# A two-layer decoder trunk: the MLP's second product by Strassen's scheme, its weight sums by adding DMAs, and the first product with the tokens in the partitions

## The chip, the cores and the metric

The kernel runs on one core of a Trainium2 chip. The metric is the device time of one execution in microseconds (us), taken as the median of several runs. TensorE (PE) multiplies, VectorE (DVE) and ScalarE (ACT) do the elementwise work, GpSimd (POOL) and SyncE (SP) mostly issue transfers. A DMA that is issued by SP is called a load here.

## The reference

256 tokens of 2048 features pass through two layers. Each layer has a mixer (gated linear attention in layer 0, windowed attention in layer 1), a cross-attention into 256 memory tokens, an output product, and an MLP; all arrays are float32. The change is in the MLP alone:

```python
def squared_relu_mlp(h, w_up, w_down):
    return jnp.square(jax.nn.relu(h @ w_up)) @ w_down
...
        x = x + squared_relu_mlp(rmsnorm(x, mlp_norm_g[i]), w_up[i], w_down[i])
```

`w_up` is 2048 x 8192 and `w_down` is 8192 x 2048, so each MLP reads 2 x 64 MB of weights.

## The kernel before, in words

Every weight is read once, in parts of 128 partitions x 1024 floats (512 KB). A part with its products is an `Item`, and the whole program is one list of items that is walked in order. In round i of the walk the load of item i + 8 is written (`load`, on SP's queue, into one of `WR` = 5 slots `wr`), then the split of item i + 3 (`split`), then the products of item i (`mm`). TensorE multiplies in a reduced form of float32, so each operand is cut into a high part and a remainder: ScalarE copies the part to `wh`, VectorE subtracts to get `wl` (four slots of each). A product of two such operands is three matmuls: high x high, high x remainder, remainder x high. As `wh` has four slots, the split of item i + 3 has to wait until TensorE is through with item i - 1.

Work that is not a product of a weight (norms, attention, transposes) sits in generators in the list `tasks`; `step_tasks` moves each of them one `yield` further in every round with products. The framework that builds the program adds all waits, and it may place an instruction on its engine elsewhere than the code has it.

The MLP of a layer runs in four quarters of 2048 hidden features. The first product has the hidden features in the partitions: `fm_halves` makes 128 of them from two items, each of 8 matmuls of 512 columns (256 tokens, high and remainder side by side) with `wh` as the weights in the array, and 8 of 256 columns with `wl`. `done` then adds the two halves (`combine`: one op of ScalarE, one of VectorE), multiplies with the norm factor, squares the positive part, and splits the result. The second product has the tokens in the partitions: `tm_halves` takes the 16 chunks of a quarter and 512 output features in 8 items of 12 matmuls each (two tiles of tokens, two chunks, three matmuls of 512 columns); at the end `add_residual` adds both banks of PSUM (the accumulators of TensorE, 8 in all: four "main", four "aux") to the residual `x`. The last 512 outputs of the last quarter are done by `last_group`, one tile of tokens after the other.

Of the kernel before, what the change touches and what calls it, by code (L numbers as in the profile page):

```python
# [28 lines left out]
# feature chunks (of 128) of the layer-0 projection, in the order of the jobs  # L29
# [20 lines left out]

class Item:
    """One load: a part of a weight with its products, or a part of an input."""

    def __init__(self, src, width, split=None, mm=None):
        self.src, self.width, self.split, self.mm = src, width, split, mm


@with_exitstack
def trunk_kernel(ctx: ExitStack, tc: tile.TileContext, a, out):
# [12 lines left out]
    # ---------------------------------------------------------------- loads  # L72
# [7 lines left out]
    gains = vec("gains", [P, 5, NK], act)     # mem, attn0, attn1, mlp0, mlp1  # L80
# [11 lines left out]
    # TensorE's clock is raised by the time the first operands are there  # L92
# [4 lines left out]
    # ------------------------------------------------------------- helpers  # L97
    def split_slot(which, name):
        return [sp.tile([P, 2 * T], F32R, tag=f"{which}{c}", name=f"{name}{c}") for c in range(NK)]

# [8 lines left out]
    class Stats:  # L109
        """1/sqrt(mean of squares + eps) of an array [token, feature]."""  # L110
# [22 lines left out]
    def spread(tok, name):  # L133
        """[token, tile] along the free axis of every partition, in PSUM."""
# [7 lines left out]
    def inv_sqrt(name, src, scale, r=None, v=None, w=None):  # L142
# [41 lines left out]
    def tm_halves(name, srcs, n, lhs, done, order=None):  # L184
        """All tokens in the partitions, n output features along the free axis."""
# [24 lines left out]
    def combine(acc, name):  # L210
        """acc's two halves added, in SBUF."""
# [6 lines left out]
    S = {}     # what later closures look up  # L218

    def put_out(c, src):  # L220
        S["os"][c] = sp.tile([P, 2 * T], F32R, tag=f"B{c}", name=f"os{c}")
# [45 lines left out]
    def x_task():  # L267
        """The residual with the tokens in the partitions."""
# [70 lines left out]
    # ---------------------------------------------------------------- layer 0  # L339
    def gla_halves():  # L340
# [29 lines left out]
        def proj_done(job, idx):  # L370
            kind, h, j = job

            def f(acc):
# [528 lines left out]
```

## Time and profile before

| what | value |
|---|---|
| time, median of 3 runs | 2143.64 us (2143.62 to 2143.68) |
| span of the profiled execution, its first to its last instruction | 2142.3 us |
| granted TensorE clock, mean over the span | 0.999 |
| read from HBM in the span | 394.52 MB |
| first product of the MLP of layer 0, first weight load into the array | 465.1 us |
| first product of layer 1's projection, first weight load into the array | 1180.8 us |

The profile describes one execution, whose own time is its span and the little before the first and after the last instruction that the profile does not show; the span is 1.3 us under the median of the runs. Busy time of TensorE counts matmuls from start to modelled end, and these overlap. The distance between the starts of equal items is therefore the better measure of what an item costs.

### The profile page before, as it was taken

The numbers are of one execution on the slowest core, as the hardware profiler recorded it, in microseconds if no ns is written. First come the engines' busy times: TensorE is split into PE (matmuls) and PEld (weight loads), VectorE is DVE, ScalarE is ACT, GpSimd is POOL, SyncE is SP. The second block draws the span as 40 slices with busy tenths as digits, with TensorE's granted clock in tenths as the row PEclk, the third lists the DMA queues.
The fourth block names the chain that finished last, engine by engine and source line by source line (L and its number), as shares of the span: only waits on it lengthen the run. The fifth ranks groups of instructions, "written<-read, shape, count | busy, mean of one in ns | idle before, by whom it ended". The sixth has DMA issues, their size and how long they took to land.

```text
span 2142.3 us, 28800 instructions
## 1 busy us (share of the span) xinstructions
PE 2129.7 (99%) x11014; PEld 1809.6 (84%) x11014; DVE 1348.5 (63%) x1971; ACT 1040.2 (49%) x1586; POOL 9.1 (0%) x26
## 2 busy tenths in 40 slices
PE   9999999999999999999999999999999999999998
PEld 9988888888888888888888887888888888888886
DVE  5655777557646656755765688567557646645673
ACT  6744666544434434434444566454444434434452
POOL 0000000000000000000000000000000000000000
PEclk9999999999999999999999999999999999999999
DMA  8855554555565555555555544555566566555572
GB/s 286 278 177 187 168 167 152 183 182 183 190 192 190 192 190 189 185 194 187 187 187 187 173 130 131 191 184 186 190 190 192 188 193 188 187 190 189 185 243 80
DMA packets 111883, 398.71 MB, mean 186 GB/s; under 512 B 12684, under 2 KB 12896, under 8 KB 111616
## 3 DMA queue, kind: packets, MB, share of 16 engines
q1 hardware_dynamic: 109872, 393.40, 56.7%
q10 hardware_dynamic: 1680, 3.38, 0.5%
q8 instruction: 86, 1.41, 0.3%
q14 instruction: 53, 0.43, 0.1%
q0 software_dynamic: 192, 0.08, 0.0%
HBM read 394.52 MB, written 2.10 MB: 185 GB/s over the span
## 4 chain that ended last, share of the span: by engine, by line
PE 99%; DMA 0%; DVE 0%; ACT 0%; SPq 0%; issue 0%; DVEq 0%
PE u_acc L175 22%; PE u_acc L176 11%; PE d_acc L203 11%; PE d_acc L202 11%; PE d_acc L201 11%; PE p_acc L175 6%; PE s_acc L175 3%; PE p_acc L176 3%; PE o_acc L201 3%; PE o_acc L202 3%; PE o_acc L203 3%; PE s_acc L176 2%; PE mk_acc L175 1%; PE v_acc L203 1%; PE v_acc L202 1%; PE v_acc L201 1%
## 5 line engine op out<-in xcount | busy, mean ns | idle before, releaser
L808 DVE TENSOR_TENSOR wl<-wr,wh 128x1024 fp32r<-128x1024 f32 (+1 forms) x734 | 890.8, 1214 | 692.9 <-ACT wh L807 691.7
L807 ACT ACTIVATE wh<-wr 128x1024 fp32r<-128x1024 f32 (+1 forms) x734 | 770.8, 1050 | 1012.6 <-issue 385.0
L175 PE MATMUL u_acc<-mx,wh 128*128 128x512 f32 x2048 | 721.0, 397 | 0.0
L176 PE MATMUL u_acc<-mx,wl 128*128 128x256 f32 x2048 | 574.8, 281 | 0.0
L175 PEld LDWEIGHTS u_acc<-mx,wh 128*128 128x128 f32 x2048 | 384.4, 188 | 92.7
L203 PE MATMUL d_acc<-wh,h 128*128 128x512 f32 x992 | 388.8, 392 | 0.0
L202 PE MATMUL d_acc<-wl,h 128*128 128x512 f32 x992 | 388.2, 391 | 0.0
L201 PE MATMUL d_acc<-wh,h 128*128 128x512 f32 x992 | 388.2, 391 | 0.0
L176 PEld LDWEIGHTS u_acc<-mx,wl 128*128 128x128 f32 x2048 | 387.1, 189 | 0.3
L202 PEld LDWEIGHTS d_acc<-wl,h 128*128 128x128 f32 x992 | 186.3, 188 | 40.8
L201 PEld LDWEIGHTS d_acc<-wh,h 128*128 128x128 f32 x992 | 186.3, 188 | 40.6
L203 PEld LDWEIGHTS d_acc<-wh,h 128*128 128x128 f32 x992 | 186.4, 188 | 40.3
L175 PE MATMUL p_acc<-ax,wh 128*128 128x512 f32 x512 | 183.8, 402 | 0.0
L176 PE MATMUL p_acc<-ax,wl 128*128 128x256 f32 x512 | 143.6, 280 | 0.0
L175 PEld LDWEIGHTS p_acc<-ax,wh 128*128 128x128 f32 x512 | 96.2, 188 | 23.7 <-ACT wh L807 1.0
L175 PE MATMUL s_acc<-ax,wh 128*128 128x512 f32 x304 | 111.3, 407 | 0.0
L201 PE MATMUL o_acc<-wh,os 128*128 128x512 f32 x256 | 100.8, 394 | 0.0
L203 PE MATMUL o_acc<-wh,os 128*128 128x512 f32 x256 | 99.6, 390 | 0.0
L202 PE MATMUL o_acc<-wl,os 128*128 128x512 f32 x256 | 99.5, 389 | 0.0
L176 PEld LDWEIGHTS p_acc<-ax,wl 128*128 128x128 f32 x512 | 96.8, 189 | 0.2
L176 PE MATMUL s_acc<-ax,wl 128*128 128x256 f32 x304 | 85.1, 280 | 0.0
L175 PEld LDWEIGHTS s_acc<-ax,wh 128*128 128x128 f32 x304 | 57.1, 188 | 15.7 <-issue 3.3
(236 smaller groups left out, 1731.8 us busy)
## 6 DMA issues: line engine op xcount, KB each, us to landing
wr<-in_w_up_dram SPq DMA_DIRECT2D x256, 512.0 KB, 4.4
wr<-in_w_down_dram SPq DMA_DIRECT2D x256, 512.0 KB, 4.4
wr<-in_w_gla_dram SPq DMA_DIRECT2D x64, 512.0 KB, 4.2
wr<-in_w_out_dram SPq DMA_DIRECT2D x64, 512.0 KB, 3.6
wr<-in_w_swa_dram SPq DMA_DIRECT2D x38, 512.0 KB, 3.7
wr<-in_w_v_dram SPq DMA_DIRECT2D x32, 388.0 KB, 4.2
wr<-in_w_mv_dram SPq DMA_DIRECT2D x16, 512.0 KB, 4.5
wr<-in_w_mk_dram SPq DMA_DIRECT2D x16, 512.0 KB, 4.3
```

The source lines that it names most:

```text
L175: pe.matmul(acc, wh[:, k * P:(k + 1) * P], rk, start=kk == 0, stop=False, skip_group_check=True)
L176: pe.matmul(acc[:, T:2 * T], wl[:, k * P:(k + 1) * P], rk[:, 0:T], start=False, stop=kk == NK - 1, skip_group_check=True)
L201: pe.matmul(acc, hi, h, start=first, stop=False)
L202: pe.matmul(acc, hi, l, start=False, stop=False)
L203: pe.matmul(acc, lo, h, start=False, stop=last)
L807: act.activation(hi[i][:, 0:w], r[:, 0:w], AF.Copy)
L808: dve.tensor_tensor(lo[i][:, 0:w], r[:, 0:w], hi[i][:, 0:w].bitcast(F32), ALU.subtract)
```

## The change

The first product now has the tokens in the partitions as well. `up(n)` makes 512 hidden features for both tiles of tokens from 8 items of 12 matmuls; ScalarE applies the norm factor and the relu (`p`). A generator, `hid_task`, then transposes the result on TensorE (8 blocks of 128 x 128 for each n, 16 n for each layer), squares it on the way out of PSUM, and, for the first seven eighths of the hidden features, makes the sums of blocks that Strassen's scheme (in Winograd's form) wants: S3, GG, S2 and S4 beside A11, A12 and A22. All seven operands of such a unit are split in one op of ScalarE and one of VectorE of 1792 elements each.

The second product runs in eighths e of 1024 hidden features (two units each). For e = 0 to 6 `down_fast(e)` makes seven products of blocks in place of eight: 7 operands x 2 units x 2 pairs of output groups are 28 items, each of 6 matmuls, where the kernel before has 16 items of 12 for the same features. Two banks per pair hold running sums for a whole layer, and after each operand one of the two banks is added to or subtracted from one block of `x` (`take`, 14 in each eighth, written two rounds with products later by `later`). The weights' sums are made in SBUF: a tile `chain` gets block B11 by a load; after its split POOL issues a DMA with `accum_op=ADD` that adds B12 to it (T1), after the next split one that adds B22 (T2), then B21 (T4). T3 is a load of B12 and an adding DMA of B22 into a slot of `wr`. Each eighth has 16 loads of 512 KB and 16 adding DMAs of 512 KB for its second product. The last eighth is done without the scheme (`down_plain`, `last_group`).

The items of the first product for the next eighth are woven into those of the second product (`woven`: 16 up items and 28 down items, the last 4 of them at the end). `WR` is 6, tiles with the tag `B` live in the pool of the phase, the pool of layer 1's mixer is opened later, and the scratch space for DMA descriptors is set to 8192. The weights are laid out anew on the host.

```diff
-WR = 5
+WR = 6
...
+A21, A11, A22, A12, S3, GG, S2, S4 = range(8)
+FAST = [(A11, "B11", 0, True, [(0, 0, 1)]),
+        (GG, "T1", 1, True, [(1, 1, -1)]),
+        (S2, "T2", 0, False, [(0, 1, -1)]),
+        (S4, "B22", 1, False, [(0, 1, -1)]),
+        (S3, "T3", 0, False, [(1, 1, -1)]),
+        (A22, "T4", 0, False, [(1, 0, 1)]),
+        (A12, "B21", 1, True, [(0, 0, 1)])]
...
         def up(n):
...
+            def part(i):
+                def mm(wh, wl):
+                    if i == 0:
+                        if n == 0:
+                            open_phase()
+                        st["acc"] = [bank("main" if n < 2 else "aux", f"u{layer}{n}_acc{t}") for t in range(2)]
+                    for t in range(2):
+                        for k in range(2):
+                            rk = S["xs"][2 * i + k]
+                            h, l = wh[:, k * 512:(k + 1) * 512], wl[:, k * 512:(k + 1) * 512]
+                            hi, lo = rk[:, t * P:(t + 1) * P], rk[:, T + t * P:T + (t + 1) * P]
+                            acc = st["acc"][t]
+                            pe.matmul(acc, hi, h, start=2 * i + k == 0, stop=False)
+                            pe.matmul(acc, hi, l, start=False, stop=False)
+                            pe.matmul(acc, lo, h, start=False, stop=2 * i + k == NK - 1)
+                    if i == 7:
+                        p = S["phase"].pool.tile([P, 2, 512], F32, tag="relu", name=f"p{layer}{n}", bufs=2)
+                        for t in range(2):
+                            act.activation(p[:, t, :], st["acc"][t], AF.Relu, scale=S["st"].tok[:, t:t + 1])
+                        making[n] = hid_task(n, p)
+                        tasks.append(making[n])
+                return Item(a["w_up"][layer, n, i], 1024, mm=mm)
...
+        def hid_task(n, p):
+            pool = S["phase"].pool
+            yield
+            yield
+            q = pool.tile([P, 8, T], F32, tag="sq", name=f"q{layer}{n}", bufs=1)
+            for o in (0, 2):
+                b = bank("aux", f"h{layer}{n}{o}")
+                for j in range(2):
+                    t, half = {A21: (1, 0), A11: (0, 0), A22: (1, 1), A12: (0, 1)}[o + j]
+                    for c in range(2):
+                        col = (2 * half + c) * P
+                        pe.transpose(b[:, j * T + c * P:j * T + (c + 1) * P], p[:, t, col:col + P], ident)
+                act.activation(q[:, o:o + 2, :].rearrange("p o c -> p (o c)"), b, AF.Square)
+            yield
+            yield
+            u = pool.tile([P, 7, 512], F32R, tag="hid", name=f"hid{layer}{n}", bufs=3)
+            if n // 2 < 7:
+                dve.tensor_tensor(q[:, S3:GG + 1, :], q[:, A11:A22 + 1, :], q[:, A21:A21 + 1, :].to_broadcast([P, 2, T]),
+                                  ALU.subtract)
+                dve.scalar_tensor_tensor(q[:, S2, :], q[:, GG, :], -1.0, q[:, A11, :], ALU.mult, ALU.subtract)
+                dve.scalar_tensor_tensor(q[:, S4, :], q[:, S2, :], -1.0, q[:, A12, :], ALU.mult, ALU.subtract)
+                first, ops = 1, 7
+            else:
+                first, ops = 0, 4
+            act.activation(u[:, 0:ops, 0:T], q[:, first:first + ops, :], AF.Copy)
+            dve.tensor_tensor(u[:, 0:ops, T:2 * T], q[:, first:first + ops, :], u[:, 0:ops, 0:T].bitcast(F32),
+                              ALU.subtract)
+            unit[n] = u
+            del making[n]
...
+            def item(idx, u, pair):
+                o, name, which, first, uses = FAST[idx]
+                def mm(wh, wl):
+                    if u == 0 and pair not in sums:
+                        sums[pair] = {}
+                    if u == 0 and which not in sums[pair]:
+                        sums[pair][which] = bank("main", f"d{layer}{e}{pair}{which}")
+                    acc = sums[pair][which]
+                    products(acc, 2 * e + u, o, wh, wl, first and u == 0, u == 1)
+                    if u == 1:
+                        def take():
+                            for t, col, sign in uses:
+                                dst = x[t][2 * pair + col]
+                                if sign > 0:
+                                    dve.tensor_tensor(dst, acc, dst, ALU.add)
+                                else:
+                                    dve.tensor_tensor(dst, dst, acc, ALU.subtract)
+                        later.append([1, take])
...
+                def plus(other):
+                    def f():
+                        pool_e.dma_start(held[pair, u], block(pair, u, other), accum_op=ALU.add)
+                    return f
+                if name == "B11":
+                    it = Item(block(pair, u, "B11"), 1024, mm=mm, held=new_tile, then=plus("B12"))
+                    it.tile = held_tile
+                    return it
+                if name == "T1":
+                    return Item(None, 1024, mm=mm, held=held_tile, then=plus("B22"))
+                if name == "T2":
+                    return Item(None, 1024, mm=mm, held=held_tile, then=plus("B21"))
+                if name == "T4":
+                    return Item(None, 1024, mm=mm, held=held_tile)
+                if name == "T3":
+                    return Item(block(pair, u, "B12"), 1024, mm=mm, plus=block(pair, u, "B22"))
+                return Item(block(pair, u, name), 1024, mm=mm)
+            return [item(idx, u, pair) for idx in range(7) for u in range(2) for pair in range(2)]
...
+        def woven(us, ds, tail):
+            hs, m = [], len(ds) - tail
+            for i, u in enumerate(us):
+                hs.append(u)
+                hs += ds[m * i // len(us):m * (i + 1) // len(us)]
+            return hs + ds[m:]
+        first, second = up(0), up(1)
+        hs = first[0:6] + second[0:6] + first[6:] + second[6:]
+        for e in range(7):
+            hs += woven(up(2 * e + 2) + up(2 * e + 3), down_fast(e), 4)
+        for g in range(4):
+            if (layer, g) == (1, 3):
+                last_group(hs, len(hs) - 8)
             else:
+                hs += down_plain(g)
...
         raw[i] = wp.tile([P, 1024], F32, tag="wr", name="wr", bufs=WR)
         nc.sync.dma_start(raw[i][:, 0:h.width], h.src)
+        if h.plus is not None:
+            pool_e.dma_start(raw[i], h.plus, accum_op=ALU.add)
...
+        if h.then:
+            h.then()
```

More of the change, by code (lines that the diff above doesn't have):

```diff
@@ L98, in split_slot @@
     def split_slot(which, name):
-        return [sp.tile([P, 2 * T], F32R, tag=f"{which}{c}", name=f"{name}{c}") for c in range(NK)]
+        pool = sp if which == "A" else S["phase"].pool
+        return [pool.tile([P, 2 * T], F32R, tag=f"{which}{c}", name=f"{name}{c}") for c in range(NK)]
     def split_scaled(dst, src, g):
@@ L693, in down, with open_phase @@
-        def down(q, g):
-            def done(accs):
-                add_residual(g, accs)
-                if q == 3:
-                    finish(g)
-            return tm_halves(f"d{layer}{q}{g}", [a["w_down"][layer, q, g, i] for i in range(8)], 512,
-                             lambda: [hid[16 * q + k] for k in range(16)], done)
+        unit = {}
+        making = {}
+        wd = a["w_down"]
+        def open_phase():
+            S["phase"].close()
+            S["phase"] = Phase(f"mlp{layer}")
+            S["st"].finish()
+            if layer == 1:
+                S["gfin"] = S["phase"].pool.tile([P, D], F32, name="gfin")
+                act.dma_start(S["gfin"], a["g_fin"])
@@ new lines, in up @@
+        def up(n):
+            st = {}
+            def part(i):
[20 more added lines that the diff above has]
+                return Item(a["w_up"][layer, n, i], 1024, mm=mm)
+            return [part(i) for i in range(8)]
@@ new lines, in operand, with products @@
+        def operand(n, o, c):
+            if n in making:
+                for _ in making[n]:
+                    pass
+            if n // 2 < 7:
+                o -= 1
+            u = unit[n]
+            return u[:, o, c * P:(c + 1) * P], u[:, o, T + c * P:T + (c + 1) * P]
+        def products(acc, n, o, wh, wl, first, last):
+            for c in range(2):
+                hi, lo = operand(n, o, c)
+                h, l = wh[:, c * 512:(c + 1) * 512], wl[:, c * 512:(c + 1) * 512]
+                pe.matmul(acc, hi, h, start=first and c == 0, stop=False, skip_group_check=True)
+                pe.matmul(acc, hi, l, start=False, stop=False, skip_group_check=True)
+                pe.matmul(acc, lo, h, start=False, stop=last and c == 1, skip_group_check=True)
@@ L745, in products @@
                 return Item(None, 0, mm=mm)
-            for i in range(8):
+            for i in range(4):
                 hs.insert(at + 3 * i, fetch(i))
-            hs += [products(t, i) for t in range(2) for i in range(8)]
+            hs += [part(t, i) for t in range(2) for i in range(4)]
         def final(t):
```

132 lines of the change are left out of this document (72 added, 60 removed).

## The prediction

> **What bounds the kernel now.** I read the page first: busy times, the slices, the chain that ended last.
>
> ```profile
> span 2142.3 us, 28800 instructions
> PE 2129.7 (99%) x11014; PEld 1809.6 (84%) x11014; DVE 1348.5 (63%) x1971; ACT 1040.2 (49%) x1586; POOL 9.1 (0%) x26
> ...
> PE 99%; DMA 0%; DVE 0%; ACT 0%; SPq 0%; issue 0%; DVEq 0%
> PE u_acc L175 22%; PE u_acc L176 11%; PE d_acc L203 11%; PE d_acc L202 11%; PE d_acc L201 11%; PE p_acc L175 6%; PE s_acc L175 3%; PE p_acc L176 3%; PE o_acc L201 3%; PE o_acc L202 3%; PE o_acc L203 3%; PE s_acc L176 2%; PE mk_acc L175 1%; PE v_acc L203 1%; PE v_acc L202 1%; PE v_acc L201 1%
> ```
>
> The chain is TensorE nearly throughout, and two thirds of it are the MLP's two products (u_acc and d_acc). Next come the waits, of ScalarE, TensorE and SP.
>
> ```profile
> ACT wh L807 <- PE d_acc L203: 351.9, 214, 1.7
> PE v_acc L201 <- ACT wh L807: 2.4, 2, 1.4
> SPq L795 <- DVE wl L808: 932.7, 400, 4.7
> ```
>
> The splits wait for TensorE to free a slot, the loads wait for the splits, and TensorE waits 2.4 us in all. So a shorter TensorE program shortens the kernel, until one of the others no longer keeps up. Last, the price of an item. ScalarE's split starts once for each item, as TensorE releases it, so the distance of these rows of the timeline (start, duration) is TensorE's time for one item.
>
> ```profile
> 545.92 1.06 ACT L807 ACTIVATE wh<-wr 128x1024 fp32r<-128x1024 f32 x1 [1.46 <-issue]
> 557.23 1.06 ACT L807 ACTIVATE wh<-wr 128x1024 fp32r<-128x1024 f32 x1 [1.46 <-issue]
> ...
> 562.85 1.06 ACT L807 ACTIVATE wh<-wr 128x1024 fp32r<-128x1024 f32 x1 [1.38 <-issue]
> 568.34 1.06 ACT L807 ACTIVATE wh<-wr 128x1024 fp32r<-128x1024 f32 x1 [1.69 <-PE d_acc L203]
> ```
>
> The first two rows lie four items of the first product apart (11.31 us): 2.827 us for each. The last two lie two items of the second product apart: 2.745 us for 12 matmuls of 512 columns, 0.229 us each. Durations of single matmuls (0.39) overlap and aren't used.
>
> **TensorE's work.** The first product has 256 items in both layers (16 n, 8 parts, 2 layers), as many as before. They go from 2.827 to 2.745: -21.1 us. The second had 256 items of 2.745, or 702.7 us. It now has 14 eighths x 28 items of 6 matmuls (1.372 each) and 32 whole items: 538.0 + 87.8 = 625.8, so -76.9 us. New are 256 transposes of 128 x 128. The chain of the layer before has the same operation, eight at a time:
>
> ```profile
> 400.23 0.87 PE mx0t L656 x8
> ```
>
> 32 groups of eight at 0.87 are +27.8 us. Together -70.2 us. One woven eighth costs TensorE 16 x 2.745 + 28 x 1.372 + 2 x 0.87 = 84.1 us; the same work costs 16 x 2.827 + 16 x 2.745 = 89.2 now. **So 5.1 us is what an eighth may lose before the change is lost**, and there are 14 of them.
>
> **VectorE and ScalarE.** Rows of the groups by line (busy us, mean ns), the last with a PSUM source and a factor per row, as the new relu has:
>
> ```profile
> L808 DVE TENSOR_TENSOR wl<-wr,wh 128x1024 fp32r<-128x1024 f32 (+1 forms) x734 | 890.8, 1214 | 692.9 <-ACT wh L807 691.7
> L807 ACT ACTIVATE wh<-wr 128x1024 fp32r<-128x1024 f32 (+1 forms) x734 | 770.8, 1050 | 1012.6 <-issue 385.0 <-PE d_acc L203 351.9 <-PE o_acc L203 81.1
> L687 DVE SCALAR_TENSOR_TENSOR u_t<-u_t 128x256 f32<-128x256 f32 x128 | 54.4, 425 | 4.4
> L642 DVE TENSOR_TENSOR x<-d_acc,x 128x512 f32<-128x512 f32 x62 | 39.8, 683 | 8.0 <-PE d_acc L203 8.0
> L727 ACT ACTIVATE fh<-wr 128x512 fp32r<-128x512 f32 x16 | 9.3, 623 | 10.8 <-DMA wr<-in_w_down_dram 10.8
> L331 ACT ACTIVATE xpt<-xt 128x512 f32<-128x512 f32 x8 | 4.7, 593 | 0.0
> L291 ACT ACTIVATE mv<-mv_acc,mem_r 128x512 f32<-128x512 f32 x4 | 2.8, 688 | 1.6 <-PE mv_acc L203 1.6
> ```
>
> The sums of a unit cost VectorE one op of 512 elements and two of 256: 0.68 + 2 x 0.42 = 1.5 us. Its ops of 1792 elements aren't in the trace. Carried on in a straight line from 512 and 1024 elements they are 2.0 us on VectorE and 1.7 on ScalarE. An eighth costs VectorE 44 splits (53.4), 14 takes (9.6) and two units (7.1): 70.1 of 84.1 us, 83%. ScalarE has 44 splits (46.2) and two units with two relus, two squares and a copy each (8.5): 65%. Neither becomes the bound by its sum. But the split of an item can start only when the item four ahead is done, and takes 1.05 + 1.21 = 2.3 us. Three small items in a row leave it 4.1 us, so 1.9 in reserve; with one item of the first product among them it is 5.5 and 3.2. What goes over the reserve, TensorE waits. Three places do:
>
> The **start of each layer** has no earlier units. Unit 0 is wanted one item of the first product after its transposes, and takes 1.2 (squares) + 1.5 + 1.7 + 2.0 = 6.4 us: 3.7 late. Unit 1 has 4.1 us of cover, and is 2.3 late. For two layers +12 us; the bounds are 0 (other products are placed ahead of it) and 21 (each chain stands behind another split).
>
> The **last unit of an eighth** is made among small items. Its subtraction and a take are 2.7 us that the next split can stand behind, 0.8 over the reserve. The unit in the middle is covered by the 3.2.
>
> The **sums T3 and T4** use the same bank one after the other, and one T4 item has only one small item behind the T3 item whose take must read the bank first. If that take stands behind a split, it ends 2.3 + 0.7 us after a start for which 1.4 us are there: 1.6 late. If it stands ahead, nothing.
>
> I take 0.8 and half of 1.6 for an eighth, and as the bound below nothing. The half rests on a row:
>
> ```profile
> 557.23 1.06 ACT L807 ACTIVATE wh<-wr 128x1024 fp32r<-128x1024 f32 x1 [1.46 <-issue]
> 558.19 0.36 ACT L213 ACTIVATE u_u<-u_acc 128x256 f32<-128x256 f32 x1
> ```
>
> Here a split of the next round stands ahead of an op that the code writes first, so ops go by when their operands are there, not by the written order alone. That is 1.6 x 14 = +22 us.
>
> **DMA.** Rows by stretch of time, the share of the 16 engines and GB/s last, and the rows of issues (KB each, us to landing):
>
> ```profile
> 10.00:30.00 20.00, 20.00 (x115) 20.00 (x114) 13.71 (x22) 14.98 (x28) 0.00 (x0) 1.00 0.99 365
> 558.00:645.00 87.00, 87.00 (x381) 71.38 (x380) 44.55 (x43) 33.72 (x34) 0.00 (x0) 1.00 0.61 192
> ...
> wr<-in_w_down_dram SPq DMA_DIRECT2D x256, 512.0 KB, 4.4
> wg<-in_wg_dram POOLq DMA_DIRECT2D x4, 17.0 KB, 4.8
> ```
>
> At a share of 0.99 loads run at 365 GB/s; the MLP now takes 192. An eighth will have 32 loads (16.8 MB) and 16 adding DMAs (8.4 MB). No adding DMA is in the trace. Its lower bound is a load of the same size (factor 1): 46 + 23 = 69 us at 365 GB/s, hidden under 84.1. The upper is twice that, since it must read its destination too: 46 + 46 = 92 us, which is no longer hidden. I take 1.5 (80.5 us, nearly full): the second read is of SBUF and not of HBM, from which the 365 come. The cover ends at a factor of 1.66.
>
> A sum must also land in time. Between one split of a `chain` tile and its next lie four small and at least two other items, 11.0 us, less 2.3 for the split itself, plus 1.9 of reserve: 10.6. From the 17 KB row, 4.8 us, and 512 KB at half of 365 GB/s beside the loads, 2.9 at factor 1 and 5.7 at 2, come 7.7 to 10.5. So I cost it at nothing, and know the cover is thin: if landing takes 2 us more than the upper value, two hand-overs in each eighth lose about 4 us, 56 in all.
>
> **Other queues.** POOL has 9.1 us of work in the whole span, and an issue there is short:
>
> ```profile
> L436 POOL DMA_DIRECT2D wg<-in_wg_dram x4 | 2.1, 514 | 203.2 <-PE pre L439 203.2
> ```
>
> At half a microsecond each, the 16 of an eighth are 8 us of its 84, and hide. SP's queue has the same 512 loads for the MLP; those of a `chain` tile wait for the split of the last sum, which is long done by then. The six slots in place of five lengthen what loads can run ahead.
>
> **Sum.** 2142.3 - 70.2 + 12 + 22 = 2106.1 for the span, and with the 1.3 us by which the median lies above it, 2107.
>
> **The rivals.** *The adding DMAs become the bound* (slower). At factor 2 an eighth lasts 92 us in place of 84.1, and its small stalls vanish in that: 14 x 7.9 = 111, so 2143.6 - 70.2 + 12 + 111 = 2196. It decides from 1.66 on; 1.88 is the point of no change. For it: 0.61 of the engines' time is already taken at 192 GB/s, and 200 of plain loads with 100 of adding ones come on top of each other. Against it: 0.99 at 365 shows that the share in the MLP has waiting in it. The Trainium skill, "Collectives: The Full Stack", section "The bandwidth ceiling: the fold count and why AG ≠ RS ≠ AR", speaks for this rival: a DMA that reduces emits two read descriptors for each chunk on one ring, so it runs at half the rate of a copy, though the addition itself is free. By that rule the factor is 2 and the time 2196; no run here shows it yet.
>
> *The written order holds after all* (slower). Then a unit's copy stands on ScalarE ahead of the next split, which waits 1.5 + 1.7 us for it and 2.0 on VectorE: 5.2 against a reserve of 1.9 at the end and 3.2 in the middle of an eighth, so 3.3 + 2.0, with 1.6 for the bank 6.9. 14 x 6.9 = 97, with 21 at the starts 2191. The row of 558.19 speaks against it.
>
> *Only the landing is late*: 2107 + 56 = 2163, slower. For it, the thin cover; against it, that the 17 KB alone need 0.05 us at 365 GB/s, so the 4.8 are fixed time, part of which the bigger transfer overlaps.
>
> *Nothing is late at all*: 2143.6 - 70.2 = 2073. For it, 2.4 us of waiting in all of TensorE's rows now; against it, VectorE at 83% where it has 63 now.
>
> **How the numbers follow.** Forecast with the stall-free case 0.56 (its own range 2073 to 2135), the adding DMAs 0.27, the written order 0.08, late landing 0.09. The range 2073 to 2205 takes in all of them; outside stay adding DMAs beyond a factor of 2 (at 3 an eighth takes 115 us, and the kernel over 2500) and a gain beyond TensorE's sum. A measurement of this kernel tells 0.2% from no change, about 4.3 us, so faster is below 2139.3 and slower above 2147.9. Of the forecast 0.54 lies below; of the DMA case 0.02 lies below and 0.03 near no change, where the factor falls between 1.66 and 1.9; the rest is above: 0.56 faster, 0.06 the same, 0.38 slower.
>
> **What would show it.** If I'm right, the chain stays TensorE at over 96%, the split rows of first-product items lie 2.745 us apart, those of small items 1.37, and an eighth takes 85 to 87 us. If the adding DMAs bind, the DMA share in the woven stretches is near 1, ScalarE's split waits for a transfer into `chain` or `wr`, and TensorE is idle behind it. If the order binds, the waits of TensorE name VectorE's `wl` or a take, with the DMA share well under 0.9. A long gap at the first small items of each layer is the start. The forecast is wrong altogether if TensorE's own items don't shrink to these prices, above all if the 6-matmul item costs more than half of a whole one.

## The result, and the profile after

The changed kernel takes 2195.52 us (median of 4 runs, 2191.18 to 2200.47) against 2143.66 before: 1.0242 times as long, with a 95% interval of 1.0228 to 1.0257. It is 52 us slower where 37 us faster was forecast. The time lies in the range that was given, and within 1 us of the price of the rival in which the adding DMAs become the bound. The experiments below show that the time does not come from where that rival has it.

The page of the profile, its header, TensorE's row, the DMA shares in 40 slices, and the chain that ended last:

```profile
span 2193.8 us, 27445 instructions
PE 2117.9 (97%) x9902; PEld 1745.5 (80%) x9902; DVE 1513.2 (69%) x1881; ACT 1251.4 (57%) x1654; POOL 200.8 (9%) x250
...
DMA  8856555568999999999996544578999999999984
...
PE 78%; DMA 13%; DVE 4%; issue 3%; ACT 2%; POOL 0%; POOLq 0%; ACTq 0%; SPq 0%; DVEq 0%
DMA wr<-in_w_down_dram 10%; PE u_acc L728 8%; PE u_acc L727 8%; PE u_acc L729 8%; PE d L786 6%; PE d L787 6%; PE d L785 6%; PE p_acc L198 5%; PE s_acc L198 3%; DVE wl L982 3%; PE p_acc L199 3%; PE o_acc L224 3%; PE o_acc L225 3%; PE o_acc L226 3%; DMA ch<-in_w_down_dram 2%
```

The chain was TensorE at 99%. Now a tenth of it is transfers into the slots `wr` of parts of `w_down`, and the DMA engines are at nine tenths or more through the woven eighths of both MLPs. What TensorE, ScalarE and SP wait for (total us, times, longest):

```profile
PE d L785 <- ACT wh L981: 53.1, 14, 4.6
PE d L786 <- DVE wl L982: 10.5, 21, 0.8
...
ACT wh L981 <- DMA wr<-in_w_down_dram: 194.6, 48, 10.0
ACT wh L981 <- DMA ch<-in_w_down_dram: 76.8, 47, 2.8
...
SPq L966 <- DVE wl L982: 1383.6, 579, 10.4
```

TensorE waits 53.1 us in 14 places: one gap for each of the 14 eighths, 2.7 to 4.6 us long and 3.8 on average, in front of a small item (L785 to L787 are its matmuls), for a split that itself waits for a transfer (L981 is the split's copy, L982 its subtraction). The chain around one of these gaps (start, duration), the row of TensorE's timeline that ends the gap (the idle time before it in brackets), and what POOL issued:

```profile
559.10 8.13 DMA wr<-in_w_down_dram
567.35 0.49 issue
567.84 10.95 DMA wr<-in_w_down_dram
578.89 1.07 ACT wh L981
579.99 1.24 DVE wl L982
581.26 0.80 PE d L786
...
585.47 0.43 PE u_acc L728
...
586.23 0.23 PE u_acc L727
```

```profile
576.24 0.80 PE L785 MATMUL d<-wh,hid 128*128 128x512 f32 x1 [2.66 <-ACT wh L981]
```

```profile
566.55 0.86 POOL L968 DMA_DIRECT2D wr<-in_w_down_dram  x1 [12.90 <-DMA wr<-in_w_down_dram]
...
1121.45 0.86 POOL L968 DMA_DIRECT2D wr<-in_w_down_dram  x1 [13.59 <-DMA wr<-in_w_down_dram]
```

L968 is the adding DMA of T3, of which an eighth has four. TensorE stops in front of the first one's products (adding DMA issued at 566.55). The chain shows the second: its load starts as a slot comes free, at 559.10, lands after 8.13 us, and only then can the adding DMA go, which takes 10.95 us. From the load to the split are 19.8 us. In the list of items the split is six items behind the one whose split freed the slot, and with four small and two whole items among them that is 4 x 1.372 + 2 x 2.745 = 11.0 us of TensorE. For the first pair they are three and three, 12.4 us, and from its load (557.96) to its split (575.13) are 17.2. The first T3 sums of six eighths in a row, 566.55 and 1121.45, are 554.9 us apart: 92.5 us for an eighth where TensorE's items alone need 84.1.

The rows also show a second price. Behind the gap, matmuls lie 0.43 us apart until some 10 us after its end; from 586.2 on they are 0.23 apart again. The same stretch by windows (the columns are stretch, length, busy time of PE, its weight loads, VectorE, ScalarE and POOL, then granted clock, DMA share and GB/s):

```profile
567.00:582.00 15.00, 11.41 (x38) 7.81 (x38) 5.30 (x7) 3.06 (x3) 2.97 (x4) 0.79 1.00 252
...
566.50:660.50 94.00, 90.41 (x385) 72.90 (x384) 68.17 (x68) 52.96 (x54) 13.66 (x16) 0.95 0.99 272
```

The granted clock falls to 0.79 in the 15 us around this gap, and to 0.974 over the span (0.999 before). By the clock's records in the trace it is halved once at each of the 14 gaps, for 3.4, 6.8 or 10.2 us. This closes the sum: -70.2 for TensorE's items, 53.1 + 10.5 - 2.4 = +61 of waits, and (0.999 - 0.974) x 2193.8 = +55 for the clock make +46, of the +51.5 by which the span grew; 5 us stay without a name.

The Trainium skill, "TensorE: Matmul & The Clock Gate", section "Part 1: The HAM clock gate", has the clock halve after at least one idle window of about 3.4 us and come back after at least one window of about 3.4 us of work. The halved stretches here are one, two or three times 3.4 us, which agrees; but a stop of 2.66 us was enough to halve the clock, and there the rows decide.

Small items cost what was put down for them (two splits of the timeline, each started by TensorE, 1.38 us apart), and the new ops of VectorE and ScalarE too (mean ns in the groups by line, each shape by itself):

```profile
684.26 1.06 ACT L981 ACTIVATE wh<-wr 128x1024 fp32r<-128x1024 f32 x1 [0.30 <-PE d L787]
685.64 1.07 ACT L981 ACTIVATE wh<-ch 128x1024 fp32r<-128x1024 f32 x1 [0.31 <-PE d L787]
```

```profile
L766 DVE TENSOR_TENSOR hid<-q,hid 128x1792 fp32r<-128x1792 f32 x28 | 56.7, 2024 | 9.8 <-ACT hid L765 9.8
L765 ACT ACTIVATE hid<-q 128x1792 fp32r<-128x1792 f32 x28 | 47.7, 1704 | 11.4 <-DVE q L761 11.4
```

And the issues (KB each, median us to landing), `ch` being the tile `chain`:

```profile
wr<-in_w_down_dram SPq DMA_DIRECT2D x200, 512.0 KB, 6.4
ch<-in_w_down_dram POOLq DMA_DIRECT2D x168, 512.0 KB, 10.4
...
wr<-in_w_down_dram POOLq DMA_DIRECT2D x56, 512.0 KB, 9.3
```

### The profile page after: what moved, and what is told of

It is laid out like the page before. It is cut to its first block, busy times and chain, and to the rows that moved or that the text cites. A ratio compares the mean times of both kernels' runs of the same rounds, so it can differ in the third digit from the quotient of the medians.

```text
span 2193.8 us, 27445 instructions
## 1 busy us (share of the span) xinstructions
PE 2117.9 (97%) x9902; PEld 1745.5 (80%) x9902; DVE 1513.2 (69%) x1881; ACT 1251.4 (57%) x1654; POOL 200.8 (9%) x250
## 4 chain that ended last, share of the span: by engine, by line
PE 78%; DMA 13%; DVE 4%; issue 3%; ACT 2%; POOL 0%; POOLq 0%; ACTq 0%; SPq 0%; DVEq 0%
DMA wr<-in_w_down_dram 10%; PE u_acc L728 8%; PE u_acc L727 8%; PE u_acc L729 8%; PE d L786 6%; PE d L787 6%; PE d L785 6%; PE p_acc L198 5%; PE s_acc L198 3%; DVE wl L982 3%; PE p_acc L199 3%; PE o_acc L224 3%; PE o_acc L225 3%; PE o_acc L226 3%; DMA ch<-in_w_down_dram 2%
## 5 line engine op out<-in xcount | busy, mean ns | idle before, releaser
L982 DVE TENSOR_TENSOR wl<-wr,wh 128x1024 fp32r<-128x1024 f32 (+1 forms) x682 | 816.3, 1210 | 423.2 <-ACT wh L981 419.4
L981 ACT ACTIVATE wh<-wr 128x1024 fp32r<-128x1024 f32 (+1 forms) x682 | 708.8, 1048 | 614.7 <-DMA wr<-in_w_down_dram 194.6
L727 PE MATMUL u_acc<-wh,mx 128*128 128x512 f32 x1024 | 403.1, 394 | 0.0
L728 PE MATMUL u_acc<-wl,mx 128*128 128x512 f32 x1024 | 401.8, 392 | 0.2
L729 PE MATMUL u_acc<-wh,mx 128*128 128x512 f32 x1024 | 401.0, 392 | 0.0
L785 PE MATMUL d<-wh,hid 128*128 128x512 f32 x784 | 323.2, 412 | 53.3 <-ACT wh L981 53.1
L982 DVE TENSOR_TENSOR wl<-ch,wh 128x1024 fp32r<-128x1024 f32 x224 | 274.3, 1224 | 141.9 <-ACT wh L981 141.5
L981 ACT ACTIVATE wh<-ch 128x1024 fp32r<-128x1024 f32 x224 | 238.2, 1064 | 231.0 <-PE u_acc L729 94.0
L786 PE MATMUL d<-wl,hid 128*128 128x512 f32 x784 | 323.3, 412 | 10.6 <-DVE wl L982 10.5
L787 PE MATMUL d<-wh,hid 128*128 128x512 f32 x784 | 315.7, 404 | 0.0
L785 PEld LDWEIGHTS d<-wh,hid 128*128 128x128 f32 x784 | 153.6, 196 | 97.5 <-ACT wh L981 63.5
L728 PEld LDWEIGHTS u_acc<-wl,mx 128*128 128x128 f32 x1024 | 194.4, 190 | 43.1 <-DVE wl L982 2.4
L727 PEld LDWEIGHTS u_acc<-wh,mx 128*128 128x128 f32 x1024 | 194.7, 190 | 41.3
L729 PEld LDWEIGHTS u_acc<-wh,mx 128*128 128x128 f32 x1024 | 193.7, 189 | 40.8
L786 PEld LDWEIGHTS d<-wl,hid 128*128 128x128 f32 x784 | 153.8, 196 | 52.8 <-DVE wl L982 22.8
L787 PEld LDWEIGHTS d<-wh,hid 128*128 128x128 f32 x784 | 154.1, 197 | 33.9 <-DVE hid L766 0.7
## 6 DMA issues: line engine op xcount, KB each, us to landing
ch<-in_w_down_dram POOLq DMA_DIRECT2D x168, 512.0 KB, 10.4
```

What stands on the lines that cost most here:

```text
L727: pe.matmul(acc, hi, h, start=2 * i + k == 0, stop=False)
L728: pe.matmul(acc, hi, l, start=False, stop=False)
L729: pe.matmul(acc, lo, h, start=False, stop=2 * i + k == NK - 1)
L785: pe.matmul(acc, hi, h, start=first and c == 0, stop=False, skip_group_check=True)
L786: pe.matmul(acc, hi, l, start=False, stop=False, skip_group_check=True)
L787: pe.matmul(acc, lo, h, start=False, stop=last and c == 1, skip_group_check=True)
```

## The experiments

Two theories were to be told apart. *Volume*: the adding DMAs move too much, and the eighth lasts as long as its transfers. *Place*: the transfers fit, but T3 is a load with an adding DMA behind it in one of six slots, and that pair can't be done in the time between a slot's release and the split. Under *place* there are two shades, that the pair starts too late, or that it holds slots which the other loads need.

**All adding DMAs as plain ones.** The same issues and bytes, without the addition.

```diff
-                        pool_e.dma_start(held[pair, u], block(pair, u, other), accum_op=ALU.add)
+                        pool_e.dma_start(held[pair, u], block(pair, u, other))
...
-            pool_e.dma_start(raw[i], h.plus, accum_op=ALU.add)
+            pool_e.dma_start(raw[i], h.plus)
```

> All 224 adding DMAs become plain DMAs of the same bytes, issued by POOL at the same places behind the same waits (the sums of weights are left out: each tile then holds the last block written). Theory V (volume: an adding DMA costs the 16 engines twice a plain one, so an eighth needs about 92 us of them): an eighth now needs 69 us, TensorE is the bound again, 85 to 87 us for an eighth, 2100 to 2125 us in all. Theory W (place: the tile of T3 needs a load and then a second transfer behind it, on POOL's in-order queue, and the six slots don't give that much lead): the pair is still one behind the other, only the landing is shorter; the gap once in an eighth shrinks but stays, 2140 to 2180 us.

Measured: 2133.60 us, 0.9955 of before (0.9937 to 0.9972), and 62 us under the changed kernel. TensorE still waits:

```profile
PE d L785 <- ACT wh L981: 19.7, 12, 2.8
```

So the addition has a price, but without it the kernel is still 60 us above TensorE's sum (2143.6 - 70.2 = 2073.4), and 12 of the 14 eighths still have a gap in front of T3's products, now those of the third pair. The time lies between the two ranges and meets neither. The gaps speak for *place*: the second transfer of T3 is late even as a plain one.

**T3 without its adding DMA.**

```diff
-                    return Item(block(pair, u, "B12"), 1024, mm=mm, plus=block(pair, u, "B22"))
+                    return Item(block(pair, u, "B12"), 1024, mm=mm)
```

> The adding DMA of T3 is left out (T3 is then B12 alone), 12 adding DMAs an eighth in place of 16. Theory V: 46 + 12 x 2.9 = 81 us of DMA for an eighth, just under TensorE's 84: 2105 to 2130 us. Theory W: the pair is gone, 2105 to 2130 us too. A time above 2150 speaks against both.

Measured: 2080.70 us, 0.9704 (0.9688 to 0.9720). 56 of 224 adding DMAs are gone, and with them 115 us; that is 24 us better than the range that both theories gave. What TensorE waits for in the MLP is down to one row:

```profile
PE u_acc L728 <- DVE wl L982: 0.3, 1, 0.3
```

The first `chain` sums of the eighths, five eighths apart:

```profile
601.89 0.86 POOL L826 DMA_DIRECT2D ch<-in_w_down_dram  x1 [48.71 <-DMA wr<-in_w_up_dram]
...
1021.68 0.86 POOL L826 DMA_DIRECT2D ch<-in_w_down_dram  x1 [47.55 <-DVE wl L982]
```

That is 419.8 us, or 84.0 for an eighth: TensorE's sum of 84.1, with nothing lost to the order. But this kernel also moves less, so it doesn't yet tell *volume* from *place*.

**T4 without its adding DMA, T3 left whole.** This leaves out as many adding DMAs as the run before, elsewhere.

```diff
-                    return Item(None, 1024, mm=mm, held=held_tile, then=plus("B21"))
+                    return Item(None, 1024, mm=mm, held=held_tile)
```

> The adding DMA that turns T2 into T4 is left out (T4 is then T2), again 12 in place of 16 for an eighth, but T3 keeps its load with the adding DMA behind it. Theory V: 81 us of DMA for an eighth as without T3's, so the same time within 15 us: 2105 to 2140 us. Theory W: the pair of T3 is as before, so the gap stays: 2180 us or more.

Measured: 2177.48 us, 1.0159 (1.0144 to 1.0174).

```profile
PE d L786 <- DVE wl L982: 29.0, 41, 0.8
PE d L785 <- ACT wh L981: 27.8, 28, 2.5
```

With the same volume it is 97 us above the run before. *Volume* can't explain that; T3's place can. (The time is 3 us under the 2180 that *place* was given, and the waits come in more and shorter pieces than in the changed kernel: all 28 of the second row stand in front of T3's products, none is over 2.5 us, and the granted clock is 0.993.)

**The transfers alone.** No trunk is computed; the same parts of 512 KB are moved, by SP alone, by POOL alone, and as two loads of SP beside one adding DMA of POOL.

```diff
+    loads(48, 0)
+    fence()
+    plain(48, 0)
+    fence()
+    adds(48, 48)
...
+    for i in range(32):
+        sp.dma_start(la[(2 * i) % 6], ups[48 + 2 * i])
+        sp.dma_start(la[(2 * i + 1) % 6], ups[49 + 2 * i])
+        pool_e.dma_start(lb[i % 6], downs[96 + i], accum_op=ALU.add)
```

> No part of the trunk is computed (the output is a copy of x): stages of 512 KB transfers by themselves, six tiles in flight on each queue: 48 loads of SP; 48 plain ones of POOL; 48 adding ones of POOL; 64 loads with 32 adding; 64 loads with 32 plain ones of POOL; six adding, six plain, six loads, each behind the one before. Theory V: adding ones alone run at 160 to 220 GB/s, half the 365 of loads, and 64 loads with 32 adding take 180 to 190 us. Theory W: adding ones run at 280 GB/s or more, and the mixed stage takes under 155 us.

Measured (windows: plain loads, then a stretch in which loads and adding DMAs alternate one to one; DMA share and GB/s last):

```profile
10.00:55.00 45.00, 3.26 (x4) 0.00 (x0) 1.00 1.03 411
...
240.00:330.00 90.00, 6.39 (x12) 20.19 (x24) 1.00 1.05 275
```

A plain part of 524288 bytes takes 1.276 us at 411 GB/s. In the mixed stretch 24 adding DMAs are issued in 90 us, one every 3.75; by the rate, a pair (1.049 MB at 275 GB/s) is 3.81. Less the plain part, the adding one takes 2.54 us: a factor of 2.0. The stages ran into one another, so the trace has no stretch of adding DMAs alone, and the expected 160 to 220 GB/s for them was not measured. The Trainium skill, "Collectives: The Full Stack", section "The bandwidth ceiling: the fold count and why AG ≠ RS ≠ AR", has two reads for one write in the rings of collectives; the factor here, within one core, agrees. An eighth's transfers are then 32 x 1.276 + 16 x 2.54 = 81.5 us, under the 84.1. It is tight, and it fits.

**T3 in tiles of its own.** Volume, sums and items are unchanged; the four T3 parts of an eighth get four tiles, so they neither wait for a slot nor hold one. Room for them comes from one relu tile less and from the final gain, which shares a slot with `q`.

```diff
+                def new_third():
+                    third[pair, u] = S["phase"].pool.tile([P, 1024], F32, tag=f"third{pair}{u}", name=f"th{layer}{e}{pair}{u}")
+                    return third[pair, u]
...
-                    return Item(block(pair, u, "B12"), 1024, mm=mm, plus=block(pair, u, "B22"))
+                    it = Item(block(pair, u, "B12"), 1024, mm=mm, plus=block(pair, u, "B22"), held=new_third)
+                    it.tile = third_tile
+                    return it
...
-                nc.sync.dma_start(h.held(), h.src)
+                z = h.held()
+                nc.sync.dma_start(z, h.src)
+                if h.plus is not None:
+                    pool_e.dma_start(z, h.plus, accum_op=ALU.add)
```

> Only the place of T3's tile changes: it gets four tiles of its own in place of slots of wr (the space comes from one buffer less of p and from reading the last gain later). Its load and its adding DMA are issued at the same places in the same order. Theory S (slots: a T3 tile holds one of the six slots for two transfers, some 16 us, so four of them leave two slots for all other loads): the gap goes or is under 1 us for an eighth, 2080 to 2110 us. Theory L (landing: eight items ahead are too little for a load and an adding DMA behind it, whoever's tile it is): the gap stays, 2150 to 2195 us.

Measured: 2089.47 us, 0.9742 (0.9725 to 0.9758). It beats both kernels, by 54 and 106 us. TensorE's waits are a few us, and the eighth with all its bytes takes (1001.16 - 488.62) / 6 = 85.4 us:

```profile
488.62 0.93 POOL L974 DMA_DIRECT2D th<-in_w_down_dram  x1 [167.82 <-DMA th<-in_w_down_dram]
...
1001.16 0.85 POOL L974 DMA_DIRECT2D th<-in_w_down_dram  x1 [20.68 <-DVE wl L995]
```

```profile
575.00:661.00 86.00, 85.41 (x382) 69.90 (x381) 67.77 (x67) 54.04 (x55) 13.65 (x16) 1.00 1.02 295
```

```profile
th<-in_w_down_dram POOLq DMA_DIRECT2D x56, 512.0 KB, 8.9
...
569.62 2.59 SPq L972 DMA_DIRECT2D th<-in_w_down_dram  x2
```

T3's adding DMA lands little faster than before (8.9 against 9.3 us), and nobody waits, because the pair starts long ahead of its use: the load of 569.62 belongs to a split at 652.66. In its own tile a T3 load goes out as soon as the split of the eighth before has read the tile, some 82 us ahead of its use. So the time met the range of the shade with the slots, but the other shade isn't out: own tiles take away the late start as well. The same transfers run at 295 GB/s in place of 272, at a DMA share of 1.02 in place of 0.99: the share was near 1 in both, and says nothing about how much more would fit. With all the bytes moved and the price gone, *volume* has fallen.

**The pair earlier still.** The load and adding DMA of T3 are written as items of their own, earlier in the list.

```diff
+            if early:
+                return [item(4, u, pair, True) for u in range(2) for pair in range(2)]
...
+            if e < 6:
+                for k, it in enumerate(down_fast(e + 1, True)):
+                    hs.insert(len(hs) - 5 + k, it)
```

> T3 in four tiles of its own as in e5_own_tiles, and its load and adding DMA are issued an eighth's end earlier, where no other adding DMA is under way. Theory S: no better than e5_own_tiles by more than 10 us. Theory L: 2080 to 2110 us, far below e5_own_tiles. If the 16 engines are simply full (32 loads at 1.28 us and 16 adding DMAs at 2.55 are 81.7 us of an eighth's 84.1), both stay above 2120.

Measured: 2090.91 us, 0.9749 (0.9735 to 0.9764), the same as the run before.

```profile
569.61 2.59 SPq L981 DMA_DIRECT2D th<-in_w_down_dram  x2
```

But the edit hardly moved the loads. They go out 11 to 16 us earlier in the first eighth of each layer, and within 1.2 us of the run before in the other twelve, as they still wait for the tile to be read. So this run says nothing about an earlier start.

**Late again, in own tiles.** This tells the two shades of *place* apart. A copy of one column by VectorE, one for each T3 load (56, not 28), ties T3's load to the split six items earlier, the moment at which a slot would have come free.

```diff
+                if h.plus is not None:
+                    k = used[-6]
+                    used.append(i)
+                    dve.tensor_copy(z[:, 0:1], lo[max(k, i - 8)][:, 0:1].bitcast(F32))
                 nc.sync.dma_start(z, h.src)
```

> T3's four sums have own tiles as in e5_own_tiles, so they hold none of the six slots, but a one-column copy on VectorE ahead of each of these loads (28 in all, well under 0.1 us each) ties it to the split six items earlier, which is when a slot would have come free for it. If what costs the time is when the pair can start (theory L: load and adding DMA behind it need some 16 to 18 us and have about 11), the gap of TensorE comes back once in each eighth, with 40 to 60 us of waits in front of T3's products, a clock of 0.97 to 0.98, and 2150 to 2200 us. If it is that the pair keeps slots from the other loads (theory S), the other loads still run ahead and the time stays at 2090 to 2110 us.

Measured: 2262.3 us, 1.055 (1.0534 to 1.0566).

```profile
PE d L782 <- ACT wh L999: 94.8, 26, 5.7
```

With the six slots free for all other loads, the tie costs 173 us over own tiles. In each eighth the gap in front of the first T3 product is back (14 gaps, 65.6 us together, against 53.1 in the changed kernel), so the late start alone is enough for it, without the slots that T3 holds. But the price is 62 us over the top of what was expected, since 12 eighths have a second gap, in front of the fourth T3 product. The rows of VectorE and SP show where it comes from:

```profile
576.82 1.22 DVE L1000 TENSOR_TENSOR wl<-th,wh 128x1024 fp32r<-128x1024 f32 x1 [10.09 <-ACT wh L999]
577.96 0.15 DVE L975 COPY th<-wl 128x1 f32<-128x1 f32 x1
```

```profile
562.71 0.86 SPq L984 DMA_DIRECT2D wr<-in_w_up_dram  x2
578.14 0.33 SPq L976 DMA_DIRECT2D th<-in_w_down_dram  x1
```

The copy for the fourth load runs right behind the subtraction of the first T3 part, which waits for the late first pair. So the fourth load starts 20 us after the first (10.5 in the changed kernel) and is late in its turn. Meanwhile SP issues nothing for 15 us, as the next load on its queue is the tied one; whether that has a price was tried next.

**The same, with T3's loads on POOL's queue**, where none of the loads of other parts stands behind them.

```diff
-                nc.sync.dma_start(z, h.src)
+                (pool_e if h.plus is not None else nc.sync).dma_start(z, h.src)
```

> As e9_pinned (T3 in own tiles, each of its loads tied to the split six items earlier), but these 56 loads are issued from GpSimd's queue in place of SP's, so that the loads behind them on SP don't stand behind a load that waits. If the late start of the pair alone sets the price, TensorE's gaps before T3's products stay as in e9_pinned (94.8 us of waits) and the time is 2230 to 2265 us. If the price is that the other loads stand behind the waiting one while the transfers run dry, most of it goes: waits under 50 us and 2090 to 2180 us, the more so as the loads that run ahead fill the time in which T3's pair can't start.

Measured: 2288.31 us, 1.0678 (1.0648 to 1.0709).

```profile
PE d L782 <- ACT wh L999: 96.8, 41, 5.5
```

Other loads can pass the waiting one now, and it didn't help: the wait at the first T3 product is there in each eighth (65.4 us), and in 12 eighths the fourth load is again tied behind the first T3 part. So SP's held queue is not what the price needs. But the run is 23 us over its range, and it exchanges one held queue for another: T3's third load is issued at 566.50 only, on POOL's queue behind an adding DMA that waits until 565.94 for its own load. How much that costs, no run tells.

**Seven slots and five** (of the changed kernel, which has six).

```diff
-WR = 6
+WR = 7
```

> The changed kernel with seven slots in place of six. Theory L: the load of T3 starts one item earlier, 1.4 to 2.7 us, of a gap of 3 to 4 us in each eighth; the waits of 64 us fall to 25 to 45, the clock gap shrinks with them, and the time is 2130 to 2165 us. If only the volume of the DMAs counted, a slot more would change nothing that lasts: 2190 to 2196 us.

> The changed kernel with five slots, as the kernel before had. Theory L: T3's load starts one item later, so each eighth loses 1.4 to 2.7 us more: 20 to 40 us more, with the other loads closer to the edge as well, 2215 to 2250 us. If only the volume of the DMAs counted: 2190 to 2200 us.

Measured: 2185.63 us with seven (1.0196, 1.0180 to 1.0211) and 2297.76 with five (1.0713, 1.0695 to 1.0731). With seven, and then with five, TensorE waits:

```profile
PE d L785 <- ACT wh L981: 41.3, 26, 3.0
```

```profile
PE d L785 <- ACT wh L981: 129.7, 28, 6.5
```

The volume is the same in all three, and the time goes from 2186 to 2298, so the slots bind. Both sizes were missed: a slot less costs 102 us and not 20 to 55, a slot more brings 10 and not 30 to 65. With five slots there are two gaps in each eighth, and the second comes about as in the tied kernel: the fourth T3 load waits for the slot that the first T3 part holds, and starts right behind its subtraction.

```profile
579.07 1.22 DVE L982 TENSOR_TENSOR wl<-wr,wh 128x1024 fp32r<-128x1024 f32 x1 [9.25 <-ACT wh L981]
...
580.32 0.33 SPq L966 DMA_DIRECT2D wr<-in_w_down_dram  x1
```

So here the slots that T3 holds do count. That the seventh brings so little fits the issues, though no run isolates it: with more loads under way a load of `w_down` lands after 7.0 us in place of 6.4 and an adding DMA into `wr` after 10.0 in place of 9.3, which takes back 1.3 us of the one item gained.

```profile
wr<-in_w_down_dram SPq DMA_DIRECT2D x200, 512.0 KB, 7.0
...
wr<-in_w_down_dram POOLq DMA_DIRECT2D x56, 512.0 KB, 10.0
```

**T3's sum on GpSimd.** No adding DMA for T3; GpSimd adds the two loaded parts, and the items of B22 and T3 alternate.

```diff
-            pool_e.dma_start(raw[i], h.plus, accum_op=ALU.add)
+            pool_e.tensor_tensor(raw[i], raw[i], kept.pop(h.plus), ALU.add)
```

> T3's sum is made by GpSimd from two tiles that are loaded anyway (B12 and B22), 12 adding DMAs for an eighth; the items of B22 and T3 alternate so that no slot is held longer than now. The computation is whole. DMA is 71.5 us for an eighth, there is no second transfer behind a load: 2078 to 2095 us, unless GpSimd's op of 1024 elements and VectorE's subtractions hold each other up, which would show as waits for wl and 2100 us or more.

Measured: 2112.36 us, 0.9853 (0.9838 to 0.9868): better than the change, 23 us behind own tiles. Two rows of the groups say why:

```profile
L991 DVE TENSOR_TENSOR wl<-wr,wh 128x1024 fp32r<-128x1024 f32 (+1 forms) x682 | 906.5, 1344 | 270.2 <-ACT wh L990 261.3 <-DMA wr<-in_w_up_dram 3.0
...
L975 POOL TENSOR_TENSOR wr<-wr 128x1024 f32<-128x1024 f32 x56 | 162.6, 2903 | 296.9 <-DMA wr<-in_w_down_dram 209.4 <-DVE wl L991 47.8 <-issue 37.9
```

The addition takes 2.9 us, and VectorE's subtraction goes from 1210 ns on average to 1344: 0.134 x 682 = 91 us more of VectorE's time, and TensorE waits 19.6 us for it. The excess lies where the two meet: the 81 subtractions that overlap an addition take 2363 ns on average and up to 3436, the other 601 take 1207.

**Only the first product.** The new first product, the transposes and the weaving, with a second product in whole items and no scheme.

```diff
-            if n // 2 < 7:
+            if False:
...
-            hs += woven(up(2 * e + 2) + up(2 * e + 3), down_fast(e), 4)
+            hs += woven(up(2 * e + 2) + up(2 * e + 3), [z for g in range(4) for z in down_mid(e, g)], 2)
```

> The first product, the transposes and the weaving stay, the second product is done plainly (16 items of 12 matmuls for an eighth, no sums and no adding DMAs). The terms of the prediction for the first product alone, -21.1 for its items and +27.8 for the transposes, give 2150 us if nothing waits: 2145 to 2160.

Measured: 2154.79 us, 1.0048 (1.0033 to 1.0063), without waits of TensorE in the MLP. The terms of this part, -21.1 and +27.8, give 2150.3; they are right to within 5 us. All that the scheme can win lies in the second product, and taken alone this part loses.

## Why the prediction was wrong

*TensorE's work* (-70.2) was right. Small items lie 1.38 us apart, an eighth takes 84.0 us where nothing waits, and the kernel with T3's addition left out ends 7 us above this sum. That remainder isn't in the eighths; where it is was not followed up.

*VectorE and ScalarE* were right in their sums: 2.02 and 1.70 us for the ops of 1792 elements (2.0 and 1.7 put down), 67.8 and 54.0 us busy in 86 with own tiles (70.1 and 55 in 84). The stalls worked out from them were too large. The *start of each layer* (+12) can be at most those 7 us, and of the 22 us for the *last unit of an eighth* and the *sums T3 and T4* nothing is seen where T3 makes no wait: the eighth is at TensorE's sum. That fits the reading that ops go by when their operands are there, better than the half of 1.6 and the 0.8 gave it credit for; no run tests it by itself. Own tiles leave 85.4 us for an eighth, inside the 85 to 87 of the forecast, but with transfers near their limit it isn't shown which of the two takes the 1.4.

*DMA*, the factor: 2.0 and not 1.5, the upper bound. But the plain rate was taken from a stretch at 365 GB/s, and the engines can do 411. Two errors cancelled, 81.5 us against the 80.5 put down, and the verdict "nearly full, hidden" held. The rival *the adding DMAs become the bound* had the right factor with the wrong rate, 92 us. Its 2196 is the measured time by coincidence: with all its volume the kernel runs in 2089. (Its point of no change, put at a factor of 1.88, leaves out the 12 us at the starts that its sum has; with them it is 1.84.) Its signs, a DMA share near 1 and ScalarE waiting for a transfer into `chain` or `wr`, were all there, and did not tell a full engine from a late one. The sign that would have is the count of TensorE's waits, one for each eighth at one item.

The step that failed is *a sum must also land in time*. It was worked out for the hand-over of a `chain` tile alone, 7.7 to 10.5 us against 10.6. That was right: the landing is 10.4 there, and those hand-overs make no gap. T3 was never put through the same step. It needs two transfers one behind the other (8.13 + 0.49 + 10.95 us in the chain above) in the 11.0 to 12.4 us that a slot of `wr` gives. The sentence under *Other queues* that six slots lengthen what loads can run ahead kept it from view: the change adds a slot, and T3's four pairs hold their slots for two transfers in place of one. (POOL's issues, put at half a microsecond, took 0.85 us; they hid all the same.) The case *only landing late* had the mechanism at 0.09, at the wrong tile and with no price for the clock: it put 56 us on stalls, and the stalls are 61.

The *clock* was in no term. The 55 us behind the gaps are nearly as much as the gaps, so stops of 3 to 5 us on this engine had to be counted about twice. Shorter stops did not: without T4's addition TensorE waits 61 us in pieces of at most 2.5, and the clock's share of the time is (0.999 - 0.993) x 2179.5 = 13 us. Some 30 us of that run's time are in neither term.

Where the start was moved (five and seven slots, the two tied kernels) the direction was as expected of a late pair in each, the amount in none. For five slots and the two ties the rows give the main reason, a fourth load that hangs on the late first pair; the small gain of the seventh slot and the excess on POOL's queue stay open.

## What to carry to other kernels

When a transfer is chained to another one, work out the landing of the chain for every tile that has one, from the moment its buffer comes free to the first use, and not only for the tile in which it is most visible. A pool of slots that was deep enough for single loads was not for pairs; a tile of its own for each pair cost 16 KB per partition and was worth 106 us here. A DMA share near 1 isn't a bound by itself: compare GB/s with what the same transfers reach alone, and look at whether the waits are everywhere or at one item.

## What the runs showed of the hardware

Where adding DMAs from HBM into SBUF alternated with plain ones, one took 2.0 times the engine time of a plain one (2.54 against 1.276 us for 512 KB), and POOL needed 0.85 us to issue one, where the same DMA without the addition took 0.53. At 14 stops of TensorE of 2.7 to 4.6 us the granted clock was halved for 3.4, 6.8 or 10.2 us each time, which cost about as much as the stops; 61 us of waits in pieces of at most 2.5 us cost 13 us of clock. An addition of 128 x 1024 floats on GpSimd took 2.9 us, and VectorE's two-operand ops that overlapped one took 2.36 us in place of 1.21; the adding DMAs did not slow them (1210 ns in the changed kernel, 1214 before).
